# A rotary-embedding kernel whose DMA issues change engines and whose first slab goes in smaller passes

## The chip, the cores and the metric

The kernel runs on one core of a Trainium2 chip. The metric is the device time of one execution in microseconds (us); three runs of the kernel before gave 161.55, 161.64 and 161.67, so the median is 161.64. A core has five engines with instruction queues of their own: TensorE (PE), VectorE (DVE), ScalarE (ACT), GpSimd (POOL) and SyncE (SP). DMAs are issued by an engine's queue (here SP's and ACT's) and are carried out by 16 DMA engines that all queues share. Engines wait for one another through semaphores.

## The reference

Each of 16 heads of 64 elements is rotated: its first half x1 and its second half x2 are mixed with tables cos and sin that depend on the position in the sequence.

```python
batch, seq, dim = x.shape            # 16, 512, 1024, float32
x = x.reshape(batch, seq, num_heads, head_dim)
x1, x2 = x[..., :half_dim], x[..., half_dim:]
rotated = np.concatenate([x1 * cos - x2 * sin,
                          x1 * sin + x2 * cos], axis=-1)
```

Input and output have 33.55 MB each; the two tables have 64 KB each.

## The kernel before

The batch is cut into 8 slabs of two batch entries. A slab is a tile of 128 partitions by 8192 float32 (4 MB): each partition holds 8 consecutive positions ("rows") of 1024 elements. Three pair buffers hold two slabs each, so slabs 0 to 5 have places of their own and slabs 6 and 7 take the places of 0 and 1 once these have been stored.

Loads are issued by SyncE in this order: slab 0, slab 1 (`load`, L65), slabs 2 and 3 together in two DMAs that take every second partition (L83), slabs 4 and 5 in one DMA (L65), and later slab 6 and slab 7 (L65, called at L168), each of which waits in SyncE's queue until the store of the slab that held its place has landed. ScalarE's queue issues the loads of the tables at the start (L78) and all stores (`store`, L69): slabs 0, 1, 2 and 3 one by one, 4 and 5 in two DMAs by alternate partitions (L162), 6 and 7 in one.

The tables are cast to bfloat16 by GpSimd (L99), spread over the 128 partitions by eight small matmuls with a 0/±1 matrix (L106), and copied out of PSUM: the table for even slabs by VectorE (L113), that for odd slabs by ScalarE (L144, recorded at L138, the line of the helper `copy`).

Each slab then goes through the same stages, in place:

- **cast**: ScalarE turns float32 into bfloat16 (`cast`, L134; recorded at L138). The result lies in the lower half of the slab's own bytes.
- **two multiplications** by VectorE (L152): the bfloat16 data by the sin part of the table into the upper half, then by the cos part in place.
- **one addition** by VectorE (L155) of the two products with the halves of each head exchanged.
- **copy back**: ScalarE turns the sum into float32 over the whole slab (L158, recorded at L138).
- **store** of the slab.

A slab goes through these stages in one pass or in several passes of a few rows. The list `passes` (L118 to L123) has two passes of 4 rows for slab 0, one of 8 rows for slabs 1 to 6, and passes of 4, 2 and 2 rows for slab 7.

ScalarE's order is written by hand: every cast and copy goes through `tc.keep_in_program_order`, which keeps the instructions given to it on an engine in the order of the program; other instructions are placed by a scheduler. The program casts the two passes of slab 0, copies the odd table, casts slab 1, and then works through the passes. Ahead of a pass's multiplications it casts so many further passes that one pass is in hand (L148): so ScalarE's queue reads cast 2, copy 1, store 1, cast 3, copy 2, store 2 and so on. With slab 6 all remaining casts, those of slab 7, are put ahead of copy 6.

Of the kernel before, what the change touches and what calls it, by code (L numbers as in the profile page):

```python
# [2 lines left out]

# [4 lines left out]


@with_exitstack  # L10
def kernel(
    ctx: ExitStack,
    tc: tile.TileContext,
    x: bass.AP,
    cos: bass.AP,
    sin: bass.AP,
    num_heads: int,
    out: bass.AP,
):
    nc = tc.nc  # L20
    P = nc.NUM_PARTITIONS

    batch, seq, dim = x.shape
    nh = num_heads
    hd = dim // nh
    half = hd // 2
    bf16 = mybir.dt.bfloat16
    f32 = mybir.dt.float32

    nb = 2  # L30
    nslabs = batch // nb
    rpp = nb * seq // P
    W = rpp * dim
    TP = seq // rpp
    TW = rpp * half

    out_flat = out.rearrange("b s h d -> b s (h d)")

    singles = ctx.enter_context(tc.tile_pool(name="singles", bufs=1))
    pairs = ctx.enter_context(tc.tile_pool(name="pairs", bufs=3))  # L40
    psum = ctx.enter_context(tc.tile_pool(
        name="psum", bufs=1, space=bass.MemoryType.PSUM))


    def view(t, offset, *dims):
        return dataclasses.replace(t, offset=t.offset + offset,
                                   ap=[t.ap[0], *[list(d) for d in dims]])

    places = [pairs.tile([P, 2 * W], f32, tag="pair", name="pair") for _ in range(3)]


    def here(s, n=1):
        return view(places[s // 2 % 3], s % 2 * W, (1, n * W))


    def there(t, s, n=1):
        return bass.AP(tensor=t.tensor, offset=t.offset + s // 2 * 2 * P * W + s % 2 * W,  # L60
                       ap=[[2 * W, P], [1, n * W]])


    def load(s, n=1):
        nc.sync.dma_start(out=here(s, n), in_=there(x, s, n))  # L65


    def store(s, n=1):
        nc.scalar.dma_start(out=there(out_flat, s, n), in_=here(s, n))  # L69


    load(0)


    cos_sb = singles.tile([TP, TW], f32, tag="cos_sb")
    sin_sb = singles.tile([TP, TW], f32, tag="sin_sb")
    for t, src in ((cos_sb, cos), (sin_sb, sin)):
        nc.scalar.dma_start(out=t, in_=bass.AP(  # L78
            tensor=src.tensor, offset=src.offset, ap=[[TW, TP], [1, TW]]))

    load(1)
    for p in range(2):
        nc.sync.dma_start(out=here(2, 2)[p::2], in_=there(x, 2, 2)[p::2])  # L83
    load(4, 2)


    pick = singles.tile([TP, 4 * P], bf16, tag="pick")
    nc.gpsimd.memset(pick, 0.0)  # L88
    for h in range(2):
        for g in range(2):  # L90
            part = view(pick, (2 * h + g) * P, (TP // 2, 2 * P // TP), (1, TP // 2))
            nc.gpsimd.affine_select(  # L92
                out=part, in_=part, compare_op=mybir.AluOpType.not_equal,
                fill=1.0 - 2.0 * g, base=-h, pattern=[[0, 2 * P // TP], [-2, TP // 2]],
                channel_multiplier=1)

    tab1 = singles.tile([TP, 2 * TW], bf16, tag="tab1")
    for i, t in enumerate((cos_sb, sin_sb)):
        nc.gpsimd.tensor_copy(out=view(tab1, i * TW, (1, TW)), in_=t)  # L99

    accs, tabs = [], []
    for h in range(2):
        acc = psum.tile([P, 2 * rpp * hd], f32, tag=f"acc{h}", name="acc")
        for i in range(2):
            for f in range(2):
                nc.tensor.matmul(  # L106
                    view(acc, i * rpp * hd + f * half, (hd, rpp), (1, half)),
                    view(pick, (2 * h + i * f) * P, (1, P)),
                    view(tab1, i * TW, (half, rpp), (1, half)),
                    start=True, stop=True)  # L110
        accs.append(acc)
        tabs.append(singles.tile([P, 2 * rpp * hd], bf16, tag=f"tab{h}", name="tab"))
    nc.vector.tensor_copy(out=tabs[0], in_=accs[0])  # L113

    passes = []  # L118
    for s in range(nslabs):
        r = 0  # L120
        for n in {0: (4, 4), nslabs - 1: (4, 2, 2)}.get(s, (rpp,)):
            passes.append((s, r, n))
            r += n  # L123


    def halves(u):
        s, r, n = u
        t = here(s).bitcast(bf16)
        return [view(t, (2 * r + i * n) * dim, (1, n * dim)) for i in range(2)]


    def cast(u):
        s, r, n = u
        copy(halves(u)[0], view(here(s), r * dim, (1, n * dim)))  # L134


    def copy(out, in_):
        tc.keep_in_program_order(nc.scalar.copy(out=out, in_=in_))  # L138


    ahead = list(passes)
    for _ in range(2):
        cast(ahead.pop(0))
    copy(tabs[1], accs[1])  # L144
    cast(ahead.pop(0))
    for i, u in enumerate(passes):
        s, r, n = u
        while ahead and len(passes) - len(ahead) < (i + 2 if s < nslabs - 2 else len(passes)):  # L148
            cast(ahead.pop(0))
        lo, up = halves(u)  # L150
        for t, a in ((up, 0), (lo, rpp * hd)):
            nc.vector.tensor_mul(  # L152
                out=t, in0=lo,
                in1=view(tabs[s % 2], a + r * hd, (hd, n), (0, nh), (1, hd)))
        nc.vector.tensor_add(  # L155
            out=up, in0=up, in1=view(lo, half, (hd, n * nh), (-half, 2), (1, half)))

        copy(view(here(s), r * dim, (1, n * dim)), up)  # L158
        if r + n == rpp:
            if s == 5:  # L160
                for p in range(2):
                    nc.scalar.dma_start(out=there(out_flat, 4, 2)[p::2], in_=here(4, 2)[p::2])  # L162
            elif s == 7:
                store(6, 2)
            elif s < 4:
                store(s)
            if s < 2:
                load(s + 6)  # L168


# [1 line left out]
_INS = ['x', 'cos', 'sin', 'num_heads']  # L172
_OUTS = [((16, 512, 16, 64), 'float32')]

_NUMBERS = {'num_heads': 16}


# [26 lines left out]
```

## Time and profile before

| | before |
|---|---|
| median of 3 runs | 161.64 us |
| profiled execution: time, span of its trace | 161.8 us, 160.0 us |
| ScalarE busy | 114.3 us (71% of the span), 24 instructions |
| VectorE busy | 107.9 us (67%), 34 instructions |
| TensorE busy | 2.0 us (1%) |
| moved by DMA | 67.24 MB, 420 GB/s in the mean |
| read from and written to HBM | 33.69 and 33.55 MB |
| cast or copy back of 8 rows (ScalarE) | 7.02 us |
| of 4 rows, of 2 rows | 3.60 us, 1.90 us |
| multiplication or addition of 8 rows (VectorE) | 4.42 us |
| of 4 rows, of 2 rows | 2.29 us, 1.22 us |
| ScalarE waits for loads of slabs | 19.8 us in 4 places |

All times in the text are us from the start of the span. The line "DMA" of the page cuts the span in 40 slices of 4 us; a digit is the mean busy share of the 16 DMA engines in tenths, where 9 stands for 90% or more. The queue q1 is that of SyncE and q10 that of ScalarE; the last figure of a queue's line is the time that its packets took, as a share of 16 engines' span. A packet is one contiguous row of a DMA: 32 KB where a DMA moves one slab, 64 KB where it moves two neighbouring ones, 1 KB for the tables. The chain of waits is followed back from the last instruction; its lines give the start, the length and what filled that time. A line of the timeline gives the start and the length of a group of consecutive instructions, the engine (ACTq is ScalarE's queue, as it issues DMAs or handles a wait), the line of the kernel, the operation, the tiles, the number of instructions and, in brackets, the idle time ahead of them and what ended it.

### The profile page before, as it was taken

Reading aid. Unit: us, or ns where it says so; the run is one execution under the profiler, and the core shown is the slowest. Engines: PE = TensorE matmul, PEld = TensorE weight load, DVE = VectorE, ACT = ScalarE, POOL = GpSimd, SP = SyncE. Lnnn points to the kernel's source line nnn. Section 1 sums busy time; section 2 is a strip of 40 time slices with the busy share of each in tenths; the row PEclk is TensorE's granted clock in tenths of the full one; section 3 lists DMA queues with packets and bytes.
Section 4 is the critical chain, followed back from the end, with each engine's and each line's share of the span. In section 5 each row is a group of like instructions: output and inputs, shape, how many; then the busy total and the mean of one; then the engine's idle time right before and its main releaser. Section 6 shows DMA issues by size and latency. Waiting matters only on the chain.

```text
span 160.0 us, 167 instructions
## 1 busy us (share of the span) xinstructions
PE 2.0 (1%) x8; PEld 1.0 (1%) x8; DVE 107.9 (67%) x34; ACT 114.3 (71%) x24; POOL 2.6 (2%) x11
## 2 busy tenths in 40 slices
PE   0001300000000000000000000000000000000000
PEld 0000100000000000000000000000000000000000
DVE  0000499999951999799889979998999998000000
ACT  3006959993089989998998999999879999500000
POOL 4000000000000000000000000000000000000000
DMA  7999999699599999999999999999997999989966
GB/s 262 401 401 410 426 491 524 262 524 524 254 401 410 606 426 393 393 393 393 467 451 393 434 483 393 401 500 410 393 590 328 524 393 393 524 360 426 524 262 262
DMA packets 1920, 67.24 MB, mean 420 GB/s; under 512 B 256, under 2 KB 384, under 8 KB 384
## 3 DMA queue, kind: packets, MB, share of 16 engines
q1 hardware_dynamic: 880, 33.55, 49.5%
q10 hardware_dynamic: 1040, 33.69, 48.7%
HBM read 33.69 MB, written 33.55 MB: 420 GB/s over the span
## 4 chain that ended last, share of the span: by engine, by line
ACT 52%; DMA 26%; issue 5%; ACTq 1%; SPq 1%; another core or an unknown queue 0%
ACT pair L138 52%; DMA pair<-in_x_dram 26%; ACTq L162 1%; ACTq L69 1%; SPq L65 0%; SPq L83 0%; ACTq L138 0%
## 5 line engine op out<-in xcount | busy, mean ns | idle before, releaser
L138 ACT CAST pair<-pair 128x8192 bf16<-128x8192 f32 (+5 forms) x22 | 112.1, 5155 | 21.9 <-DMA pair<-in_x_dram 19.8
L152 DVE TENSOR_TENSOR pair<-pair,tab 128x8192 bf16<-128x8192 bf16 (+2 forms) x22 | 71.4, 3259 | 9.3 <-ACT pair L138 8.9
L155 DVE TENSOR_TENSOR pair<-pair 128x8192 bf16<-128x8192 bf16 (+2 forms) x11 | 35.8, 3260 | 0.3
L113 DVE CAST tab<-acc 128x1024 bf16<-128x1024 f32 x1 | 1.2, 1225 | 18.3 <-PE acc L106 18.3
L138 ACT ACT_TABLE_LOAD x1 | 1.3, 1283 | 2.0 <-issue 2.0
L106 PE MATMUL acc<-tab,pick 64*128 64x256 bf16 x8 | 2.0, 403 | 17.1 <-POOL tab L99 17.1
L106 PEld LDWEIGHTS <-pick 64*128 64x128 bf16 x8 | 1.0, 127 | 17.6 <-issue 15.6
L92 POOL TENSOR_SCALAR_AFFINE_SELECT pick<-pick 64x128 bf16<-64x128 bf16 x4 | 1.1, 303 | 0.1
L138 ACT CAST tab<-acc 128x1024 bf16<-128x1024 f32 x1 | 1.0, 1004 | 0.0
L99 POOL CAST tab<-cos_sb 64x256 bf16<-64x256 f32 x1 | 0.4, 391 | 9.5 <-DMA cos_sb<-in_cos_dram 9.5
L88 POOL MEMSET pick<- 64x512 bf16 x1 | 0.5, 519 | 0.3 <-POOLq L185 0.3
L99 POOL CAST tab<-sin_sb 64x256 bf16<-64x256 f32 x1 | 0.4, 396 | 4.9 <-DMA sin_sb<-in_sin_dram 4.9
L185 POOL MEMSET const-float32-0.0<- 128x1 f32 x1 | 0.1, 104 | 0.2 <-issue 0.2
L185 POOL MEMSET const-bfloat16-1.0<- 128x1 bf16 x1 | 0.1, 107 | 0.0
L185 POOL MEMSET const-uint8-127<- 128x1 uint8 x1 | 0.1, 107 | 0.0
L185 POOL MEMSET const-float32-1.0<- 128x1 f32 x1 | 0.1, 104 | 0.0
## 6 DMA issues: line engine op xcount, KB each, us to landing
pair<-in_x_dram SPq DMA_DIRECT2D x4, 4096.0 KB, 22.5
out_dram<-pair ACTq DMA_DIRECT2D x4, 4096.0 KB, 32.8
cos_sb<-in_cos_dram ACTq DMA_DIRECT2D x1, 64.0 KB, 11.1
sin_sb<-in_sin_dram ACTq DMA_DIRECT2D x1, 64.0 KB, 15.8
pair<-in_x_dram SPq DMA_DIRECT2D x3, 42.2
out_dram<-pair ACTq DMA_DIRECT2D x3, 21.0
```

What stands on the lines that cost most here:

```text
L69: nc.scalar.dma_start(out=there(out_flat, s, n), in_=here(s, n))
L88: nc.gpsimd.memset(pick, 0.0)
L92: nc.gpsimd.affine_select(out=part, in_=part, compare_op=mybir.AluOpType.not_equal, fill=1.0 - 2.0 * g, base=-h, pattern=[[0, 2 * P // TP] ...
L99: nc.gpsimd.tensor_copy(out=view(tab1, i * TW, (1, TW)), in_=t)
L106: nc.tensor.matmul(view(acc, i * rpp * hd + f * half, (hd, rpp), (1, half)), view(pick, (2 * h + i * f) * P, (1, P)), view(tab1, i * TW, ( ...
L113: nc.vector.tensor_copy(out=tabs[0], in_=accs[0])
L138: tc.keep_in_program_order(nc.scalar.copy(out=out, in_=in_))
L152: nc.vector.tensor_mul(out=t, in0=lo, in1=view(tabs[s % 2], a + r * hd, (hd, n), (0, nh), (1, hd)))
L155: nc.vector.tensor_add(out=up, in0=up, in1=view(lo, half, (hd, n * nh), (-half, 2), (1, half)))
L162: nc.scalar.dma_start(out=there(out_flat, 4, 2)[p::2], in_=here(4, 2)[p::2])
L185: nc = _bacc.Bacc("TRN2", target_bir_lowering=False, num_devices=1)
```

## The change

Four things change together.

- The engines that issue DMAs are exchanged: all loads of slabs are issued by ScalarE's queue, the tables and all stores by SyncE's.
- Slab 0 goes in passes of 4, 2 and 2 rows and slab 1 in two passes of 4. At the start all three passes of slab 0, the odd table and the first half of slab 1 are cast or copied; the second half of slab 1 is cast only after the last copy of slab 0 (the condition `while s and ...`). The DMAs of slab 0's store follow that last copy.
- VectorE's instructions and all DMAs of slabs but the first loads of slabs 2 and 3 now also go through `tc.keep_in_program_order`.
- The load of slab 6 stands in the program behind the store of slab 2, that of slab 7 behind the addition of slab 4 and ahead of slab 4's copy back. Before they stood behind the stores of slabs 0 and 1, on SyncE's queue.

What is computed, the tiles and the sizes of the DMAs stay as they are.

```diff
     def load(s, n=1):
-        nc.sync.dma_start(out=here(s, n), in_=there(x, s, n))
+        tc.keep_in_program_order(
+            nc.scalar.dma_start(out=here(s, n), in_=there(x, s, n)))
     def store(s, n=1):
-        nc.scalar.dma_start(out=there(out_flat, s, n), in_=here(s, n))
+        tc.keep_in_program_order(
+            nc.sync.dma_start(out=there(out_flat, s, n), in_=here(s, n)))
...
     for t, src in ((cos_sb, cos), (sin_sb, sin)):
-        nc.scalar.dma_start(out=t, in_=bass.AP(
+        nc.sync.dma_start(out=t, in_=bass.AP(
...
     for p in range(2):
-        nc.sync.dma_start(out=here(2, 2)[p::2], in_=there(x, 2, 2)[p::2])
+        nc.scalar.dma_start(out=here(2, 2)[p::2], in_=there(x, 2, 2)[p::2])
...
-        for n in {0: (4, 4), nslabs - 1: (4, 2, 2)}.get(s, (rpp,)):
+        for n in {0: (4, 2, 2), 1: (4, 4), nslabs - 1: (4, 2, 2)}.get(s, (rpp,)):
...
-    for _ in range(2):
+    for _ in range(3):
         cast(ahead.pop(0))
     copy(tabs[1], accs[1])
     cast(ahead.pop(0))
     for i, u in enumerate(passes):
         s, r, n = u
-        while ahead and len(passes) - len(ahead) < (i + 2 if s < nslabs - 2 else len(passes)):
+        while s and ahead and len(passes) - len(ahead) < (i + 2 if s < nslabs - 2 else len(passes)):
             cast(ahead.pop(0))
         lo, up = halves(u)
         for t, a in ((up, 0), (lo, rpp * hd)):
-            nc.vector.tensor_mul(
+            tc.keep_in_program_order(nc.vector.tensor_mul(
                 out=t, in0=lo,
-                in1=view(tabs[s % 2], a + r * hd, (hd, n), (0, nh), (1, hd)))
+                in1=view(tabs[s % 2], a + r * hd, (hd, n), (0, nh), (1, hd))))
-        nc.vector.tensor_add(
-            out=up, in0=up, in1=view(lo, half, (hd, n * nh), (-half, 2), (1, half)))
+        tc.keep_in_program_order(nc.vector.tensor_add(
+            out=up, in0=up, in1=view(lo, half, (hd, n * nh), (-half, 2), (1, half))))
+        if s == 4:
+            load(7)
         copy(view(here(s), r * dim, (1, n * dim)), up)
         if r + n == rpp:
             if s == 5:
                 for p in range(2):
-                    nc.scalar.dma_start(out=there(out_flat, 4, 2)[p::2], in_=here(4, 2)[p::2])
+                    tc.keep_in_program_order(nc.sync.dma_start(
+                        out=there(out_flat, 4, 2)[p::2], in_=here(4, 2)[p::2]))
             elif s == 7:
                 store(6, 2)
             elif s < 4:
                 store(s)
-            if s < 2:
-                load(s + 6)
+            if s == 2:
+                load(6)
```

## The prediction

> **What bounds the kernel now.** I read the page first (sections 2 and 3), then the packet records of the two DMA queues, then the chain of waits, then ScalarE's timeline.
>
> ```profile
> span 160.0 us, 167 instructions
> ...
> DMA  7999999699599999999999999999997999989966
> ...
> q1 hardware_dynamic: 880, 33.55, 49.5%
> q10 hardware_dynamic: 1040, 33.69, 48.7%
> ```
>
> The queues hold the 16 DMA engines for 49.5 + 48.7 = 98.2% of the span, VectorE and ScalarE are busy 67% and 71%. The packet records say it more sharply: on each engine the first data packet starts at 1.73 to 2.14 us, the last ends at 158.46 to 158.85, and between them no engine has a gap over 32 ns. A 32 KB packet takes 1.21 us and a 64 KB one 2.42 us, whether loads or stores run, alone or taking turns. So the span is one full **DMA line**: 2.1 us of start, some 157 of packets, 1.1 of end. Only a hole that opens in the line, or one that closes, can move the time.
>
> There is one hole-like loss: the load packet ahead of the very first store packet took 3.03 us in the mean of the 16 engines instead of 2.42, so 0.61 us went there. And there is one place without reserve: the last store, issued at 138.21. On one engine (number 12) its first packet waited 32 ns and began at 139.05, 0.84 us after the issue; on the others the packet before it ended later than that. Engine 15, which ends last, was free for it at 139.53. In the first load its packet began 0.21 us after engine 12's, so it needed the store by 139.26: **0.27 us of reserve**. From there the end follows the issue of the last store one for one.
>
> What sets that issue is the chain of waits:
>
> ```profile
> 2.20 42.22 DMA pair<-in_x_dram
> ...
> 44.49 1.95 ACT pair L138
> 46.45 4.97 issue
> 51.42 7.03 ACT pair L138
> ...
> 73.16 0.23 another core or an unknown queue
> ...
> 73.41 13.95 ACT pair L138 x2
> ```
>
> ```profile
> 37.30 0.35 ACTq L69 DMA_DIRECT2D out_dram<-pair  x1
> ...
> 73.41 13.94 ACT L138 CAST pair<-pair 128x8192 bf16<-128x8192 f32 x2 [0.62 <-DMA pair<-in_x_dram]
> 87.38 0.34 ACTq L69 DMA_DIRECT2D out_dram<-pair  x1
> 87.77 27.78 ACT L138 CAST pair<-pair 128x8192 bf16<-128x8192 f32 x4 [0.41 <-ACT pair L138]
> 115.58 1.22 ACTq L162 DMA_DIRECT2D out_dram<-pair  x2
> 116.83 21.34 ACT L138 CAST pair<-pair 128x4096 bf16<-128x4096 f32 x7 [1.29 <-issue]
> 138.21 0.34 ACTq L69 DMA_DIRECT2D out_dram<-pair  x1
> ```
>
> ScalarE is unbroken from 73.41 to 138.17 but for its own store issues, and at 73.41 it waited for slabs 4 and 5 to land (0.62 us). That landing is the last word of the loads on the end.
>
> **The change, part by part.**
>
> *Head: passes 4, 2, 2 of slab 0 and half of slab 1.* The durations are by tile: 3.60 (4 rows), 1.90 (2 rows) and 1.00 (table) on ScalarE, 2.29 and 1.22 on VectorE. Starts follow at 3.51 and 1.80 where nothing is waited for; a VectorE instruction that needs the one before starts after 2.33 or 1.26. ScalarE: casts at 13.35, 16.86, 18.66, table 20.46 to 21.46, half of slab 1 at 23.24 (landing as now) to 26.85. VectorE, from 19.58: rows 0-3 done at 26.53, 4-5 at 30.18, 6-7 at 33.84. Copies back: 26.75, 30.26, and 33.88 to 35.78. Store 0 is issued by SyncE at 35.82 instead of 37.30: 1.48 us earlier. Then cast 1b 35.7 to 39.3, copy 1a done at 44.4, just before slab 2 can be cast; copy 1b takes 3.6 us where copy 1 took 7.0, so store 1 goes about 3.4 us sooner than 58.47. This shortening meets no bound: ScalarE is again ahead of the landing at 73.4 (VectorE ends slab 2 at about 64.9, its copy ends at 71.95).
>
> *What the earlier store 0 does to the loads.* This is the term of the sum. In the packet records loads and stores take strict turns. Store 0, issued at 37.30, sent its first packet on engine 0 at 42.37; the load packet that began at 39.35 still went first, so about 64 KB are committed ahead. Load 7 shows the same: issued at 90.35, two 32 KB store packets that began at 91.94 and 93.15 went first, it came at 94.36. With 2.42 us committed and 0.5 to 0.84 us from issue to engine, store 0 issued at 35.82 arrives at 36.3 to 36.7, before the load packet that begins at 36.93, and so takes its turn ahead of the last packet of slabs 2 and 3: one turn earlier. From then on one more store packet, 1.21 us, stands ahead of every landing until the queue of loads runs out: slabs 2 and 3 at about 45.7 instead of 44.4, slabs 4 and 5 at 74.60 instead of 73.39. Bounds: 0 if it misses the turn by the 0.2 to 0.6 us that it has, 1.21 if it catches it; I take 1.21. The 0.61 us loss at the first store I keep as it is (bounds: gone, or doubled).
>
> The Trainium skill (DMA: Bandwidth & Descriptors, section Queues, rings and completion order) has each engine go round its queues and switch at packet boundaries. By that alone store 0 would have come in at 39.35 now and at 36.93 after the change; the trace has 42.37 now, so it disagrees on the commitment, but one turn earlier, +1.21, comes out either way.
>
> *Stores leave ScalarE.* From cast 4 to the last store it is 138.21 - 73.41 = 64.80 us now. Store 3 leaves a gap of 0.41 and stores 4/5 one of 1.29; with both gone each join also overlaps by 0.09, and the join at copy 7a by 0.10: 64.80 - 0.50 - 1.38 - 0.10 = 62.82 on ScalarE alone. But then VectorE is late: fixed in order, its 2- and 4-row passes wait each for the one before (2.33, 1.26), and it ends 62.27 after cast 4, as late as now (135.66 - 73.41 = 62.25). Copy 7c (1.90) has to follow: last store at 64.25 after cast 4, a gain of only 0.55.
>
> *Loads on ScalarE's queue.* Load 6 stands behind copy 2 and waits for store 0; load 7 behind cast 5 and waits for store 1; behind them in the queue stand cast 4 and copy 4. What matters is whether the queue reaches them early:
>
> ```profile
> L69 ACTq EVENT_SEMAPHORE  x1: 17/17/17, 46.4 to 46.4; - x1
> ```
>
> This wait belongs to store 1 (L69) and was done at 46.4, while cast 2 ran (44.49 to 51.5) and copy 1, which stands before it, had not begun (51.42). So the queue runs ahead of the compute. Load 6 then goes when store 0 has landed (now 37.30 + 32.4 = 69.7; copy 2 ends later) and load 7 when store 1 has (now 58.47 + 31.8 = 90.3), as from SyncE, and cast 4 and copy 4 (due at 73.4 and 94.2) see nothing of it. I take 0; if the cover fails it is the third rival. Load 7 takes 23.0 us to land, so at 113.3, and the cast that needs it is due at about 115.0 to 116.2.
>
> *Queues swapped at the start, tables on SyncE.* Both queues issue their first DMA at 0.74 now, and do so again; 0.
>
> The Trainium skill (same page, section Issuing engines are not separate DMA queues) says that a change of issuer only moves the sequencer's issue time. By that the swap itself is worth the gaps above and no bandwidth; q1 and q10 alternating at 1.21 and 2.42 us agree.
>
> **Sum.** Cast 4 at 74.62, last store at 74.62 + 64.25 + 0.02 = 138.89, so 0.68 later than 138.21; less the reserve of 0.27 the line opens by **0.41 us**. The profiled execution took 161.8 (span 160.0 and 1.8 around it), 0.16 above the median of 161.64; its own would be 162.2, the median **162.05**. Its own range is 161.4 (first-store loss gone: -0.61 on all) to 162.65 (doubled).
>
> **Rivals.**
> 1. *Store 0 misses the turn.* Then the landings stay, cast 4 is at 73.41, the last store at 137.66, 0.55 early; the line is full as before: 161.6, not slower. For it: the margin is only 0.2 to 0.6 us and no row fixes where in a packet the choice falls. Against: 64 KB fits both starts above. It decides if store 0 reaches the engines after 36.93. That the scheduler does not move store 0 forward ends here too.
> 2. *The first-store loss goes*, with rival 1: the store, arriving early, is ready when its turn comes. The first store packets begin at 42.28 to 42.79 whatever the phase of their engine, as if bound by their own start. The line shrinks by up to 0.61, slabs 4 and 5 land as much sooner, the last store keeps up: 161.0, faster. Against: the first load packets also took 1.88 instead of 1.21, so a first packet may cost this in any case.
> 3. *The loads hold ScalarE's queue until the compute before them ends.* Load 7 at 94.3, or at 95.5 with the lost turn, lands 23.0 later at 117.3 or 118.5, past the 115.0 to 116.2 at which cast 7a is due; the last store is 21.3 after: 138.6 or 139.8, against the 138.48 that the line allows: 161.8 to 163.0. It decides if load 7 is issued after 94.2 (138.48 - 21.3 - 23.0). The row at 46.4 speaks against it.
>
> **Chances.** Forecast 0.50, rivals 0.22, 0.12 and 0.11, and 0.05 for something slower that I don't see (ScalarE's table load of 1.28 us ahead of the first load would give 162.9). A measurement of this kernel can tell about 0.2%, 0.32 us, from no change. Slower by more: 0.32 of the forecast's 0.50 (its 0.41 is just over the bound), 0.08 of rival 3, 0.05: 0.45. Faster: 0.11 of rival 2, 0.02 each of rival 1 and the forecast: 0.15. Same: 0.40. The range from 161.0 to 163.0 takes in all three rivals and leaves out under 2 in 10.
>
> **What would show it.** Store 0 issued near 35.8 (head). Slabs 4 and 5 cast at 74.6 and not 73.4 (the turn). Load 7 issued near 90 (queue ahead) and no idle time before cast 7a. Last store near 138.9, and in the last third of the DMA row a dip ahead of it. A last store before 138.5 with no dip makes the forecast wrong and rival 1 right; a span under 159.7 speaks for rival 2.

## The result and the profile after

The changed kernel takes **162.21 us** in the median of 11 runs (162.00 to 162.52); the kernel before, run beside it on the same chip, takes 161.67 us (11 runs, 161.55 to 162.05). The ratio is 1.0025, with a 95% interval of 1.0015 to 1.0034: slower by 0.54 us, where the forecast had 0.41. The profiled execution took 162.52 us with a span of 160.7, so it is the longest of the 11; against before's profiled one (161.8 and 160.0) the span grew by 0.7. Some runs of e3, e7, e8 and e9, and of the kernel before beside the experiments, were up to 3% longer than the rest; the ratios, and the medians given for e7, e8 and e9, leave these out.

The page of the changed kernel, the same lines as before:

```profile
span 160.7 us, 187 instructions
...
DMA  6999999699799999999999999999996996969966
...
q10 hardware_dynamic: 880, 33.55, 49.3%
q1 hardware_dynamic: 1040, 33.69, 48.5%
```

The queues have changed names (q10 now has the loads) and hold the engines for 97.8% of the span instead of 98.2%. The row of digits is a poor witness here: 6s stand in it ahead of the end (at 120, 132 and 140 us), but before's row has a 6 and a 5 at 28 and 40 us, where the packet records have no gap. Holes are read from the packet records alone.

ScalarE's timeline, of which the lines around the change and the tail are kept:

```profile
23.64 8.92 ACT L141 CAST pair<-pair 128x4096 bf16<-128x4096 f32 x3 [1.83 <-DMA pair<-in_x_dram]
...
66.48 7.02 ACT L141 CAST pair<-pair 128x8192 f32<-128x8192 bf16 x1 [3.04 <-DVE pair L159]
69.84 0.34 ACTq L67 DMA_DIRECT2D pair<-in_x_dram  x1
74.93 20.86 ACT L141 CAST pair<-pair 128x8192 bf16<-128x8192 f32 x3 [1.43 <-DMA pair<-in_x_dram]
90.38 0.34 ACTq L67 DMA_DIRECT2D pair<-in_x_dram  x1
95.70 40.19 ACT L141 CAST pair<-pair 128x8192 f32<-128x8192 bf16 x9
137.26 1.90 ACT L141 CAST pair<-pair 128x2048 f32<-128x2048 bf16 x1 [1.37 <-DVE pair L159]
```

SyncE's timeline, the stores:

```profile
36.23 53.00 SPq L72 DMA_DIRECT2D out_dram<-pair  x4
116.58 1.18 SPq L168 DMA_DIRECT2D out_dram<-pair  x2
139.18 0.34 SPq L72 DMA_DIRECT2D out_dram<-pair  x1
```

Four readings. Store 0 leaves at 36.23 (37.30 before). Slabs 4 and 5 are cast from 74.93 on, 1.52 later than before, and ScalarE waits there for their load (1.43). From there to the last store it is 139.18 - 74.93 = 64.25 us, with one wait of 1.37 for VectorE's last addition. So the last store leaves 0.97 later than before, and the span is 0.7 longer: 0.97 less the reserve of 0.27 on which the prediction counted.

The packet records show both ends of it: where the turn was lost, and the hole. The records don't name the DMA engine; a packet is put to the engine on which the packet before it ended as this one began, and the numbers of the engines are only labels. Start, length and size in KB of consecutive packets (ld a load, st a store):

```
engine 9, after    ld 37.35+2.89 (64)  st 40.23+1.21 (32)  ld 41.44+2.91 (64)  st 44.34+1.21 (32)
engine 0, after    ld 37.04+2.42 (64)  ld 39.46+3.34 (64)  st 42.79+1.21 (32)
engine 10, before  ld 37.27+2.42 (64)  ld 39.69+3.11 (64)  st 42.79+1.21 (32)

engine 0, after    st 137.11+2.42 (64)  139.55 end of that DMA, 0.52 of nothing, st 140.08+2.45 (64)
```

In after, 6 of the 16 engines sent their first store packet one turn sooner (39.68 to 40.23, as engine 9), the other ten at 42.46 to 42.87 as before. The loads of slabs 4 and 5 end at 73.03 to 73.35 on the six and at 71.47 to 71.88 on the ten (71.29 to 71.80 in before). Before the last store the engines have a gap of 0.54 us in the mean, and all take it up at 140.01 to 140.16.

### The profile page after: what moved, and what is told of

Read it like the earlier page. It is cut to its first block, busy times and chain, and to the rows that moved or that the text cites. A ratio compares the mean times of both kernels' runs of the same rounds, so it can differ in the third digit from the quotient of the medians.

```text
span 160.7 us, 187 instructions
## 1 busy us (share of the span) xinstructions
PE 2.0 (1%) x8; PEld 1.0 (1%) x8; DVE 109.1 (68%) x40; ACT 114.6 (71%) x28; POOL 2.6 (2%) x11
## 4 chain that ended last, share of the span: by engine, by line
DVE 31%; DMA 27%; ACT 21%; issue 3%; another core or an unknown queue 3%; ACTq 1%
DMA pair<-in_x_dram 27%; DVE pair L156 22%; ACT pair L141 21%; DVE pair L159 8%; ACTq L67 1%; ACTq L86 0%; ACTq L141 0%
## 5 line engine op out<-in xcount | busy, mean ns | idle before, releaser
L156 DVE TENSOR_TENSOR pair<-pair,tab 128x8192 bf16<-128x8192 bf16 (+2 forms) x26 | 72.3, 2781 | 9.0 <-ACT pair L141 8.5
```

Of the source, the lines that this page charges most:

```text
L156: tc.keep_in_program_order(nc.vector.tensor_mul(out=t, in0=lo, in1=view(tabs[s % 2], a + r * hd, (hd, n), (0, nh), (1, hd))))
```

## The theories

**Turn theory** (the prediction's): what costs time is only that store 0 takes a turn of 1.21 us ahead of the loads. That delays cast 4, cast 4 delays the last store by way of a fixed chain of 64.25 us, and as nothing else is left to move, the line stands open until it comes. The rivals: the exchange of queues costs (loads in ScalarE's queue, tables beside loads); the passes or VectorE's fixed order cost by themselves; the loss at the first store changes.

## The experiments

In all of them "cast 4" is the start of the cast of slabs 4 and 5.

**e1: queues alone.** The changed kernel with before's passes and order of casts; the exchange of queues and VectorE's order stay.

```diff
-        for n in {0: (4, 2, 2), 1: (4, 4), nslabs - 1: (4, 2, 2)}.get(s, (rpp,)):
+        for n in {0: (4, 4), nslabs - 1: (4, 2, 2)}.get(s, (rpp,)):
...
-    for _ in range(3):
+    for _ in range(2):
...
-        while s and ahead and len(passes) - len(ahead) < (i + 2 if s < nslabs - 2 else len(passes)):
+        while ahead and len(passes) - len(ahead) < (i + 2 if s < nslabs - 2 else len(passes)):
```

> The change without its passes: queues exchanged, loads 6 and 7 and VectorE's fixed order as in the changed kernel, but slab 0 in two passes of 4 rows and slab 1 in one, cast as in the kernel before. Theory of the turn: store 0 is issued near 37.7, so no engine lets it in ahead of the last packet of slabs 2 and 3; cast 4 at 73.7 (before 73.41 plus the 0.3 by which the changed kernel's first load landed later), last store at 73.7 + 64.25 = 137.95, the line stays full: 161.5 to 161.8. Rival that the exchange of queues costs (first load later): 162.0 to 162.3. Rival that VectorE's fixed order at the end costs: also 162.0 to 162.3, with the last store near 139.

161.67 us, ratio 0.9997 (0.9987 to 1.0008). Store 0 left at 37.52, no engine let it in early, cast 4 began at 73.31, the last store left at 137.56 and the line has no gap:

```profile
73.31 20.86 ACT L141 CAST pair<-pair 128x8192 bf16<-128x8192 f32 x3 [1.15 <-DMA pair<-in_x_dram]
...
137.56 0.34 SPq L72 DMA_DIRECT2D out_dram<-pair  x1
```

The exchange of queues costs nothing that shows, and it brings the 0.55 us of the tail that the prediction gave it (73.31 + 64.25 = 137.56), which the full line does not turn into time. One caution: the profiled execution was the longest of the twelve (162.34, span 160.5). 14 of the 16 engines end by 158.76, as in before, but two end at 159.35 and 159.38, because single packets of theirs between 73 and 109 us took 0.15 to 0.39 longer. e9's profiled execution (span 160.5) shows the like. So the span of one profile can move by 0.5 us without a hole, and what a version is worth is read from its median, its cast 4 and its gaps together.

**e2: passes alone.** The kernel before with the new passes, order of casts and VectorE order, but its own queues and places of loads 6 and 7.

```diff
-        for n in {0: (4, 4), nslabs - 1: (4, 2, 2)}.get(s, (rpp,)):
+        for n in {0: (4, 2, 2), 1: (4, 4), nslabs - 1: (4, 2, 2)}.get(s, (rpp,)):
...
-    for _ in range(2):
+    for _ in range(3):
...
-        while ahead and len(passes) - len(ahead) < (i + 2 if s < nslabs - 2 else len(passes)):
+        while s and ahead and len(passes) - len(ahead) < (i + 2 if s < nslabs - 2 else len(passes)):
...
```

> The passes of the changed kernel (4, 2, 2 for slab 0; 4, 4 for slab 1; VectorE in fixed order) with the queues of the kernel before: loads on SyncE, tables and stores on ScalarE. Theory of the turn: the first load lands at 13.35 as before, store 0 is issued near 35.85, 1.4 to 1.5 ahead of before, and all or nearly all 16 engines let it in one turn earlier; cast 4 at 74.6; ScalarE's store issues are back in the tail, so the last store comes near 74.6 + 64.75 = 139.4 and the time is 162.3 to 162.7, slower than the whole change. Rival that the exchange of queues costs: 161.5 to 161.8.

163.19 us, ratio 1.0084 (1.0070 to 1.0099): the sign as expected, the size 0.5 to 0.9 over it. ScalarE's timeline:

```profile
36.03 0.36 ACTq L69 DMA_DIRECT2D out_dram<-pair  x1
...
74.36 13.94 ACT L138 CAST pair<-pair 128x8192 bf16<-128x8192 f32 x2 [1.36 <-DMA pair<-in_x_dram]
...
139.26 0.34 ACTq L69 DMA_DIRECT2D out_dram<-pair  x1
```

The turn is there (14 of 16 engines early, cast 4 at 74.36), and the tail is 139.26 - 74.36 = 64.90, as the store issues still stand in ScalarE's queue. The span is 160.8, so 0.8 over before's: 1.05 of later last store less 0.27 of reserve, 0.78. The rest lies outside the span: about 2.15 us there instead of the 1.8 of before. Why, no run here tells.

**e3 and e7: the second half of slab 1 first.** The changed kernel, but this half is cast ahead of slab 0's last copy, so that store 0 leaves late again while all else stays.

```diff
-        while s and ahead and len(passes) - len(ahead) < (i + 2 if s < nslabs - 2 else len(passes)):
+        while i > 1 and ahead and len(passes) - len(ahead) < (max(i + 2, 5) if s < nslabs - 2 else len(passes)):
```

> The whole change, but the second half of slab 1 is cast ahead of slab 0's last copy, so that store 0 leaves near 37.9 instead of 36.23. Theory of the turn: no engine lets it in early, slabs 4 and 5 are cast at 73.7 instead of 74.93, the last store comes at 138.0 and the time is 161.5 to 161.8. Rivals (queues, VectorE's order at the end): nothing changes, 162.0 to 162.3.

e3 did not decide: its runs lie from 161.55 to 166.46 us, the ratio is 1.0012 (0.9974 to 1.0050), and its profiled execution, of 165.19, is one of the longer ones. So the same kernel ran again:

> The third run once more, since its times scattered: store 0 near 37.7. Theory of the turn: no engine lets it in early, slabs 4 and 5 are cast at 73.4 to 73.7, last store 137.7 to 138.0, time 161.5 to 161.9. Rivals: 162.0 to 162.3.

161.76 us in the median (161.68 profiled); the ratio is 0.9993 (0.9953 to 1.0033). Store 0 left at 37.89, no engine was early, and ScalarE's timeline has

```profile
73.29 20.86 ACT L141 CAST pair<-pair 128x8192 bf16<-128x8192 f32 x3 [1.12 <-DMA pair<-in_x_dram]
...
135.62 1.90 ACT L141 CAST pair<-pair 128x2048 f32<-128x2048 bf16 x1 [1.37 <-DVE pair L159]
```

Compare these with the changed kernel's 74.93 and 137.26. The passes, the queues and VectorE's order are all there, only store 0 leaves 1.66 later, and cast 4 and the last copy come 1.64 sooner. One turn is 1.21 of that; the loss at the first store, smaller here (0.19 in the mean of the engines, 0.77 in the changed kernel), goes the same way. The interval of the time is wide and doesn't part e7 from the changed kernel (1.0015 to 1.0034); the timeline and the full line do, and e9 repeats the step with a clear time.

**e4: the tables behind the first load.** The changed kernel with the tables' loads on ScalarE's queue, behind that of slab 0, to see whether SyncE's issue beside ScalarE's spreads the first packets (1.75 to 2.67 in the changed kernel's profile, 1.73 to 2.14 in before's).

```diff
-        nc.sync.dma_start(out=t, in_=bass.AP(
-            tensor=src.tensor, offset=src.offset, ap=[[TW, TP], [1, TW]]))
+        tc.keep_in_program_order(nc.scalar.dma_start(out=t, in_=bass.AP(
+            tensor=src.tensor, offset=src.offset, ap=[[TW, TP], [1, TW]])))
```

> The whole change, but the two tables are issued by ScalarE's queue behind the first load instead of by SyncE beside it. Tests the later start alone: if SyncE's issue beside ScalarE's spreads the first load, the first packets start within 0.4 us of one another again (0.92 in the changed kernel, 0.41 before) and the first cast is back at 13.35. The tables come up to 1.2 us later, and with them VectorE's start. If store 0 then still leaves before 36.2, the turn is lost on most engines and the time is 161.9 to 162.3; if it leaves after 36.5, it is not and the time is 161.5 to 161.8.

162.26 us, ratio 1.0032 (1.0021 to 1.0042), and the spread stayed: 1.76 to 2.56. So that idea fell; e2, with before's queues, has 1.73 to 2.64 as well. Yet the first cast began at 13.08 (13.69 in the changed kernel), so the spread is not what sets it. The run shows something else. The table was ready sooner (copied out at 15.05 instead of 18.66), so store 0 left at 34.16, 2.07 us ahead of the changed kernel's. All 16 engines let it in early, yet by one turn only: first packets at 39.96 to 40.36, cast 4 at 74.57, last store at 138.82. Two microseconds sooner within one turn change nothing.

**e5: the last store in two.** The changed kernel; the last store, of slabs 6 and 7, is split into one for each.

```diff
-            elif s == 7:
-                store(6, 2)
-            elif s < 4:
+            elif s != 4:
                 store(s)
```

> The whole change, but the last store goes in two: slab 6 as soon as it is copied back (near 130.6), slab 7 at the end. Theory of the turn: slabs 4 and 5 are still cast near 74.6 to 74.9 and the last issue is still near 139, but the line has slab 6's packets until about 149, so nothing opens and the time is that of the full line, 161.5 to 161.8. Rival that the later loads or the exchanged queues cost by themselves: still 162.0 to 162.3.

162.01 us, ratio 0.9996 (0.9969 to 1.0024), the profiled run 161.81 with a span of 160.0. Its stores and its cast 4:

```profile
36.21 52.55 SPq L72 DMA_DIRECT2D out_dram<-pair  x4
116.12 1.19 SPq L168 DMA_DIRECT2D out_dram<-pair  x2
130.14 8.92 SPq L72 DMA_DIRECT2D out_dram<-pair  x2
```

```profile
74.47 20.86 ACT L141 CAST pair<-pair 128x8192 bf16<-128x8192 f32 x3 [1.33 <-DMA pair<-in_x_dram]
```

The turn is lost on all 16 engines and cast 4 is late, but slab 6's store at 130.14 fills the line while slab 7 is finished, and it has no gap. The time alone doesn't decide here: 162.01 is 0.2 over the 161.5 to 161.8 expected and at the lower end of what the rival had, and its interval overlaps the changed kernel's. It is the profile that speaks for the theory, and e10 and e11 below, where the same edit is worth 1.5 us. The turn costs time only through the last store.

**e6: passes alone, store 0 held.** e2 with store 0 issued behind the first copy of slab 1.

```diff
         copy(view(here(s), r * dim, (1, n * dim)), up)
+        if (s, r) == (1, 0):
+            tc.keep_in_program_order(store(0))
+            load(6)
...
```

> The passes with the queues of before (as the second run, 163.19), but ScalarE's queue issues store 0 only behind the first copy of slab 1, near 41 instead of 36. Theory of the turn: the store comes in behind all packets of slabs 2 and 3, slabs 4 and 5 land one turn earlier than before (72.2, two turns earlier than in the second run), the last store is issued near 137 and the time is that of the full line, 161.5 to 161.8: a store issued 5 us later makes it 1.5 us faster. Rival that the passes cost by their smaller instructions: stays near 163.

164.18 us, ratio 1.0119 (1.0071 to 1.0166): the time was missed by more than 2 us, though the step that I looked at came out (cast 4 at 72.52).

```profile
72.52 13.94 ACT L138 CAST pair<-pair 128x8192 bf16<-128x8192 f32 x2 [0.41 <-DMA pair<-in_x_dram]
...
117.45 21.23 ACT L138 CAST pair<-pair 128x4096 bf16<-128x4096 f32 x7 [2.80 <-DMA pair<-in_x_dram]
138.71 0.34 ACTq L69 DMA_DIRECT2D out_dram<-pair  x1
```

Store 0 left at 41.18, so it landed late, and load 6, which waits for it, was issued at 72.56 instead of 69.69 in e2. By then the loads' queue had run empty: its last packet before load 6 ended at 70.73, the next began at 76.84 (71.80 and 73.71 in before). Store packets at 75.6 to 76.6 and load packets at 85.2 to 87.9 us took up to 1.87 and 2.47 us instead of 1.21, 0.5 to 2 us to an engine, the engines were busy for up to 159.0 us in all (157.7 in after), and cast 7a waited 2.80 for slab 7. Store 0 has a due time on both sides. That an empty queue stretches packets is my reading of this one run; no other run tries it.

**e8: a small store ahead.** The kernel before with a store of 8 KB at 1.99 us, to a place in slab 7's output that the last store writes again, to see whether the loss at the first store is that of opening a path.

```diff
+    warm = singles.tile([P, 16], f32, tag="warm")
+    nc.gpsimd.memset(warm, 0.0)
+    nc.scalar.dma_start(out=bass.AP(
+        tensor=out_flat.tensor, offset=out_flat.offset + 3 * 2 * P * W + W,
+        ap=[[2 * W, P], [1, 16]]), in_=warm)
     load(1)
```

> The kernel before with one more store of 8 KB (zeros into slab 7's place in the output, overwritten later) issued by ScalarE behind the tables. It asks what the 0.6 us are that the packet ahead of the first store loses. If the path of the stores has to be opened once and this costs nothing while the loads run, the stretched packet at 39.3 is gone and the time is 161.0 to 161.3. If opening costs the same wherever it falls, the stretch moves to about 6 us and the time stays at 161.6 to 161.8. If it is a matter of the large store, the stretch stays at 39.3 and so does the time.

161.90 us in the median, ratio 0.9995 (0.9967 to 1.0023). The loss at slab 0's store stayed: 0.66 us in the mean of the engines (0.63 in before, counted the same way). So it is not paid once, with whatever store comes first.

**e9: passes with before's queues, the second half of slab 1 first.** e2 with the edit of e7.

> The passes with before's queues, but the second half of slab 1 is cast ahead of slab 0's last copy, so slab 0's store is issued near 37.7 again, where the first run of before's queues with the passes had 36.03. Turn theory: the store no longer reaches any engine a turn earlier, slabs 4 and 5 begin their cast near 73.4, the last store is issued near 137.7, and the time is 161.6 to 161.9, some 1.4 us under the 163.19 of the passes with before's queues. Rival (the passes themselves, or their fit with before's queues, cost the time): slabs 4 and 5 still begin near 74.4 and the time stays at 162.8 to 163.3.

161.94 us in the median (161.68 to 162.49), 0.04 over what was expected; ratio 1.0010 (0.9981 to 1.0039). Store 0 at 37.62, no engine early, cast 4 at 73.34, the last store at 138.10 and no gap in the line: one cast put elsewhere takes 1.25 of e2's 1.4 us over before away, and the two intervals (0.9981 to 1.0039 here, 1.0070 to 1.0099 in e2) are far apart. Its tail is 64.76, as in before and e2, and it too has 2.0 us outside the span.

**e10 and e11: store 0 much earlier, without and with the split.** The changed kernel with the first half of slab 1 cast behind store 0 and no additions on slab 0; e11 has e5's edit as well.

```diff
     copy(tabs[1], accs[1])
-    cast(ahead.pop(0))
...
-        tc.keep_in_program_order(nc.vector.tensor_add(
-            out=up, in0=up, in1=view(lo, half, (hd, n * nh), (-half, 2), (1, half))))
+        if s:
+            tc.keep_in_program_order(nc.vector.tensor_add(
+                out=up, in0=up, in1=view(lo, half, (hd, n * nh), (-half, 2), (1, half))))
```

> The changed kernel without VectorE's additions on slab 0 (work left out: slab 0's output holds only the products) and with the first half of slab 1 cast behind slab 0's store, so that this store is issued near 30, some 6 us before the changed kernel's. Turn theory: the store's packet then goes in three turns of 1.21 us ahead of where before had it; if each turn costs the loads behind it once, slabs 4 and 5 begin their cast near 77.0 (73.41 in before, 74.62 forecast for one turn), the last store is issued near 141.3, and the time is 164.2 to 164.7. Rival (the loads lose one turn at most, because only the packet that the store meets is put back and slab 1's cast also comes later): slabs 4 and 5 near 74.6 and 162.0 to 162.4.

> The same early store, slab 0 without its additions (work left out: slab 0's output holds only the products), with the last store split into one for slab 6 and one for slab 7. Turn theory: the line stays full, because slab 6's store is there while slab 7 is still being worked on, so that the later cast of slabs 4 and 5 (near 77.0) is covered and the time is 161.6 to 162.2, some 2.3 us under the same kernel with the last store whole. Rival (a store ahead of loads costs the line itself something): the time stays over 163.5.

e10 took 163.39 us, ratio 1.0096 (1.0066 to 1.0127), e11 161.88, ratio 1.0003 (0.9980 to 1.0025). ScalarE's cast 4 and SyncE's last store in e10, then the stores of e11:

```profile
75.68 13.94 ACT L141 CAST pair<-pair 128x8192 bf16<-128x8192 f32 x2 [1.37 <-DMA pair<-in_x_dram]
```

```profile
31.77 58.20 SPq L72 DMA_DIRECT2D out_dram<-pair  x4
117.32 1.16 SPq L168 DMA_DIRECT2D out_dram<-pair  x2
139.93 0.34 SPq L72 DMA_DIRECT2D out_dram<-pair  x1
```

```profile
131.53 8.91 SPq L72 DMA_DIRECT2D out_dram<-pair  x2
```

Store 0 left at 31.77, not near 30, and all engines sent it two turns ahead of before's (first packets at 37.49 to 37.81), not three; so cast 4 came at 75.68 and not at 77.0, and the time missed its bounds for the same reason. By turns it fits: no turn 73.29 to 73.41 (before, e1, e7, e9), one 74.36 to 74.57 (e2, e4, e5; 74.93 in the changed kernel, with its larger loss at the first store), two 75.68 and 75.85 (e10, e11), so about 1.2 us each. The rival, one turn at most, had 74.6 and falls. The gaps before the last store grow to 1.63 us in the mean of the engines in e10 (0.54 in the changed kernel), and with the split, in e11, they are gone and 1.5 us of the time with them.

## Why the prediction was right, point by point

- **The full line and its reserve.** Right. (Where the prediction says that engine 15 "needed the store by 139.26", 139.26 is when the store could have reached it; it was free at 139.53, and the difference is the reserve.) From the issue of the last store to the end of the span it is 21.52 to 21.58 us in after, e2, e4 and e10, where it came too late. Where it left by 138.21 (before, e1, e7, e9) there is no gap to speak of. The reserve of 0.27 fits: +0.97 of store gave +0.7 of span in after, +0.61 gave +0.4 in e4.
- **Head.** Store 0 at 36.23 instead of 35.82. The durations held, but slab 0's last load packet ended at 13.03 instead of 12.65, so the first cast began at 13.69 instead of 13.35, and the first half of slab 1 waited for its landing until 23.64, not 23.24. The loads' first packets are spread wider than in before, but that alone isn't the cause: with the same spread the first cast came at 13.41 in e2 and 13.08 in e4. It stays open. Store 1 left at 56.55, 1.9 us sooner and not 3.4: slab 2, which ScalarE casts ahead of slab 1's last copy, came at 46.00 instead of 44.49. Nothing hung on that.
- **The turn.** The term of 1.21 was right, but that it came at all was in part luck. Over all runs with an early store, the store reached the engines about 0.93 to 1.0 us after its issue, where I had 0.5 to 0.84, and it went in behind the load packet that began next. With 36.23 + 0.95 = 37.2 only six engines, those whose packet began at 37.23 to 37.64, let it in early; those that began at 37.00 to 37.16 did not. By the prediction's own sign (rival 1 if store 0 reaches the engines after 36.93) it looked lost: store 0 left 0.41 later and was up to half a us longer on its way than I had it, and came at 37.2. It met the turn only on engines whose packets happened to begin late. Six were enough: a cast starts when all 16 have landed. The Trainium skill (DMA: Bandwidth & Descriptors, section Why a DMA increments its semaphore by 16 and not by 1) says that each engine of a DMA adds its own count when its data has landed, and only the full count means all of it; the trace agrees, cast 4 began 1.58 us after the last of the six (73.35) and 3.05 after the last of the ten (71.88); in before it began 1.61 after the last of all 16 (71.80).
- **The loss at the first store, kept as it is.** Roughly: 0.77 in the mean of the engines of after, 0.63 in before. But on the engine that decided, it came twice, 0.47 ahead of its own first store and 0.49 on the load packet at 41.44, while the ten others met theirs; in before the deciding engine lost 0.69 once. This 0.27 and a start 0.16 later (2.03 against 1.87), less 0.09 of other differences, make the 0.34 by which its load ended later than the turn alone gives (73.35 - 71.80 - 1.21). This is what is over the forecast: 74.93 instead of 74.62, 139.18 instead of 138.89. e4, where the loss was 0.44, has 74.57 and 138.82.
- **The tail.** Right: 64.25 us from cast 4 to the last store in after, e1, e4, e5 and e7 (the sum had 0.02 on top). VectorE's fixed order eats the rest of what ScalarE gains, visible as the 1.37 before the last copy.
- **Loads on ScalarE's queue, queues exchanged.** Cost nothing, as said. Load 6 was issued at 69.84 while the copy of 66.48 to 73.5 ran, load 7 at 90.38 within the casts of 74.93 to 95.8, and e1 as a whole is at 0.9997. That rules out the third rival.
- **The other rivals.** Store 0 did miss the turn on ten engines, as the first rival had it, but for its outcome that would have had to happen on all 16; e7 is that rival made true, and it has the line full. The second (the loss goes, 161.0) has no run for it: where the loss was small (0.18 in e1, 0.19 in e7, 0.02 in e11), the time was still 161.7 to 161.9. The packet records show one reason: there the load packets of 3 to 20 us took longer instead, 0.51, 0.53 and 0.88 us more in the mean of the engines than at 1.21 each, against 0.32 in before. So the loss had in good part come earlier and not gone; what moves it, no run here tells.

The sign that I named, a dip in the DMA row, was badly chosen: it doesn't tell a hole from the way in which long packets are booked to slices.

Not settled: what sets the loss at the first store, and the time outside the span, 1.8 us in before, after and e1 and 2.0 to 2.2 in e2, e6 and e9. No version beat both kernels: those with a full line lie at 161.7 to 162.0, where before is.

## What to carry to other kernels

Where the transfers are the bound, a store that is ready sooner is not a gain by itself: it goes ahead of loads that stand in the queue, a whole turn at a time, and if it does so on a few of the 16 engines (six here), the load is late as a whole. Ask what the delayed load leads to, follow that chain to the last store, and compare it with the moment at which the line would run empty. Splitting the last store so that a part of it is ready sooner gives the line something to carry: with two turns lost it took back 1.5 us (e11 against e10), with one the hole closed (e5), though the 0.2 us of the median are too few to count.

## What the runs showed of the hardware that I had not expected

- From issue to the engines a store took 0.93 to 1.0 us here (bounds from after, e2, e5, e6 and e10, by which load packets still went first), twice what I had taken as the lower end. Where the line stood open, before the last store, it took 0.83 to 0.98 us (139.18 to 140.01 and 140.16).
- A DMA's reach is uneven: one store can be a turn early on 6 engines and not on 10, by 0.07 us in the phase of their load packets (37.16 against 37.23).
- The loss at the first store runs from 0.02 us (e11) to 0.77 (after) and goes neither with the queue nor with an earlier small store. Where it is small, load packets before 20 us lose more (0.88 us in e11, 0.32 in before).
- Holding store 0 back by 5 us was worse than a lost turn: 164.18 us in e6 against 163.19 in e2. That the empty queue of loads is the reason is not shown.
